# Hybrid decoder layer: transposes and pool matmuls put in groups behind the next stage, TensorE's order written out

## The chip, the cores and the metric

The kernel runs on one core of a Trainium2 chip. Its time is the device time of one execution in microseconds (us); the time of a version is the median of several runs. Five engines work side by side, each through its own queue of instructions in order: TensorE (PE), which multiplies matrices, with its weight loads (PEld) listed apart; VectorE (DVE); ScalarE (ACT); GpSimd (POOL); and SyncE (SP), which issues most loads. An instruction waits at the head of its queue until what it reads is there and what it overwrites is free, and holds up all that stands behind it on that engine.

## What is computed

One decoder layer on 256 tokens of width 2048. The part that matters here, cut from the reference:

```python
h = rms_norm(x, g_mix)
z_pool, z_q, z_kv, z_kr, z_mq = split(h @ w_in)
y_pool = pool_mixer(z_pool, w_pool, pool_scale)    # windowed means, then 4 matrices 128x128
q  = rms_norm(z_q, g_q_lat) @ w_q_up               # 8 heads x (128 plain + 64 rotated)
kv = rms_norm(z_kv, g_kv_lat) @ w_kv_up            # 8 heads x (128 key + 128 value)
# queries and keys: RMS norm per head, rotary part rotated, causal attention
y = concat(y_pool, y_mla, y_mem) @ w_o
x = x + y
x = x + conv_glu_ffn(rms_norm(x, g_ffn))
```

The time is mostly the feed-forward part behind it, which is not edited.

## The kernel before

All matrices are float32. Each weight and each activation is split into a high and a low part, and a product is made of three matmuls. ACT casts the high part of a weight (`wh`, line 98), DVE subtracts it to get the low part (`wl`, line 99), so each chunk of weights passes ACT, then DVE, then PE. Loaded weights (`wr`) have three places, `wh` and `wl` four each. In PSUM there are two sets of four buffers, `psm` for projections and `psa` for the rest.

The stage that is edited lies between the latent projections and the attention scores, at 126 to 182 us of the profile. It runs in the order of lines 643 to 664: `pool_in(0)`, `q_up(2)`, `pool_in(1)`, `kv_up(0)`, `pool_in(2)`, `q_up(0)`, `pool_in(3)`, `pool_mix`, `q_up(1)`, `kv_up(1)`, and then the output projection with the attention heads beside it.

- `pool_in(g)` (lines 539 to 544) projects one of four pool groups: 32 matmuls of line 124, then ACT copies half of the result (line 495), DVE adds the other (line 496) and scales it (line 544).
- `q_up(n)` and `kv_up(n)` (lines 586 and 616) project the latents: 24 matmuls each (lines 159 to 161), token-major. For each half of the tokens (`tt`) ACT copies the result to a tile `tok` and squares it (line 245), DVE sums the squares per head (line 246). Rotated queries (`q_up(2)`) then go through `rotate`, three DVE instructions per half of the rotation (lines 582 to 584). Keys (`kv_up(0)`) are scaled by DVE with their norm (lines 634 to 639). `kv_up(1)` makes the values, which ACT only copies (line 627).
- `to_features` (line 248) turns a finished `tok` tile into feature-major form: four transposes on PE (line 252) into one `psa` buffer, then a copy by ACT (lines 256, 260) or DVE (line 258).
- `pool_mix` (line 547) makes the windowed sums on DVE (lines 553 to 560), and for each group one matmul with the pool weights (line 562) whose result is split by ACT (line 171) and DVE (line 172) into `cat`, the input of the output projection.

`tok` tiles have three places (line 210). The order on each engine is set when the kernel is built: a scheduler places each instruction where it expects its inputs to be ready, except those given to `keep` (line 88), which stay in the order in which they were written among themselves. In this stage only `pool_in(0)` and the heads' matmuls are kept; the transposes, the pool matmuls and the projections around them are placed by the scheduler. So a group of transposes may stand in the middle of another projection's matmuls.

Of the kernel before, what the change touches and what calls it, by code (L numbers as in the profile page):

```python
# [11 lines left out]
F32 = mybir.dt.float32  # L12
# [6 lines left out]
P = 128  # L19
T = 256  # L20
NT = 2
D = 2048
KD = D // P
# [37 lines left out]
def layer(ctx, tc, xT_d, xn_d, memT_d, vec_d, tab_d, w_z_d, w_mqkr_d, w_q_d, w_kv_d, w_mem_d, w_pool_d, w_o_d,  # L61
          w_g_d, w_u_d, w_dn_d, out_d):
    nc = tc.nc
# [8 lines left out]
    def nm(s):  # L72
        uid[0] += 1
        return f"{s}_{uid[0]}"
# [4 lines left out]
    def ps_aux():  # L79
        return psa.tile([P, 512], F32, tag="a", name=nm("psa"))  # L80
# [7 lines left out]
    def keep(ins, on=True):  # L88

        return tc.keep_in_program_order(ins) if on else ins  # L90
# [18 lines left out]
    def gemm_t(ps, raw, o, act, ks, first=True, last=True, kept=False, between=None):  # L109


        ks = list(ks)
        nk = HS // P
        cs = range(0, len(ks), nk)
        for c in cs:
            kc = ks[c:c + nk]

            hi, lo = split_w(raw, o + c * P, len(kc) * P, shift=16 if c // nk % 2 else 48)

            for low in ((False, True) if c // nk % 2 == 0 else (True, False)):  # L120
                for i, k in enumerate(kc):
                    w = (lo if low else hi)[:, i * P:(i + 1) * P]
                    out, m = sides(ps, act(k), low)
                    keep(nc.tensor.matmul(out, w, m,  # L124
                                          start=first and c + i == 0 and not low,
                                          stop=last and c == cs[-1] and i == len(kc) - 1 and low == (c // nk % 2 == 0),
                                          skip_group_check=True), kept)
            if between is not None and c == 0:
                between()
# [51 lines left out]
    identf = const.tile([P, P], F32, name="identf")  # L181
# [14 lines left out]
    mp = mix.enter_context(tc.tile_pool(name="mix", bufs=1))  # L196
# [7 lines left out]
    def sm(n):  # L204
        o = so[0]
        so[0] += n
        return small[:, o:o + n]

    def tok():
        return mp.tile([P, 512], F32, tag="tok", name=nm("tok"), bufs=3)  # L210

    def s4():
        return mp.tile([P, 4, T], F32, tag="s4", name=nm("s4"), bufs=2)
# [31 lines left out]
        nc.scalar.activation(s3, src, AF.Square)  # L245
        nc.vector.tensor_reduce(dst, s3, axis=AX.X, op=ALU.add)

    def to_features(dst, src, tt, n, scale=None, eng=None, bank=ps_aux):

        ps = bank()  # L250
        for i in range(n):
            nc.tensor.transpose(ps[:, i * P:(i + 1) * P], src[:, i * P:(i + 1) * P], identf[:])
        d = dst[:, :, tt * P:(tt + 1) * P]
        p3 = ps[:, :n * P].rearrange("p (i t) -> p i t", t=P)
        if scale is not None:
            nc.scalar.activation(d, p3, AF.Copy, scale=scale)
        elif eng == "v":
            nc.vector.tensor_copy(d, p3)
        else:
            nc.scalar.copy(d, p3)  # L260
# [3 lines left out]
    xg = mp.tile([P, KD, 2 * T], F32R, tag="cat", name="xg")  # L264
# [13 lines left out]
    ps = ps_aux()  # L278
# [25 lines left out]
    for c in range(KD // 2):  # L304
        raw = raw0 if c == 0 else load_w(w_mem_d[c], STG, HS if c == 1 else STG)
# [4 lines left out]
        for i in range(2):  # L310
            k = 2 * c + i
# [3 lines left out]
        if c % 2:  # L315
            h = slice(2 * c - 2, 2 * c + 2)
# [5 lines left out]
    ps = ps_aux()  # L322
# [23 lines left out]
    gqk = sm(2)  # L346
# [38 lines left out]
    for c in range(KD // 2):  # L385
        raw = load_w(w_mqkr_d[c], 2 * 576)
# [97 lines left out]
    def mem_steps(m):  # L484
        if m == 0:
            mq_done()
        for h, step in beside.get(m, ()):
            (mem_heads[h].score, mem_heads[h].turn, mem_heads[h].values)[step]()
        if m == 6:
            latent_scales()  # L490
# [8 lines left out]
    zl = mp.tile([P, 6, 2 * T], F32R, name="zl")  # L499
# [4 lines left out]
    for m in range(6):  # L504
        raw = load_w(w_z_d[m], STG)
        if m in (1, 3):
            keep(nc.sync.dma_start(x1n[:, m // 2, :], xn_d[m // 2]))
        ps = ps_main()
# [6 lines left out]
        else:  # L515
            t = mp.tile([P, T], F32, tag="hadd", name=nm("zsq"), bufs=3)
# [21 lines left out]
    zp = mp.tile([P, 4, T], F32, name="zp")  # L538
    def pool_in(g):
        raw = load_w(w_z_d[6 + g], STG)  # L540
        ps = ps_main()
        gemm_t(ps, raw, 0, lambda k: xg[:, k, :], range(KD), kept=g == 0, between=lambda: mem_steps(6 + g))
        half_add(zp[:, g, :], ps)
        nc.vector.tensor_tensor(zp[:, g, :], zp[:, g, :], rxb[:], op=ALU.mult)


    def pool_mix():
        wp = tok()
        nc.scalar.dma_start(wp[:], w_pool_d)
        cur, w = zp, 1  # L550
        for g in range(4):
            nxt = s4()
            nc.vector.tensor_copy(nxt[:, g:4, 0:w], cur[:, g:4, 0:w])
            nc.vector.tensor_tensor(nxt[:, g:4, w:T], cur[:, g:4, w:T], cur[:, g:4, 0:T - w], op=ALU.add)
            cur = nxt
            w *= 2
            s = cur[:, g, :]
            e = TAB["edge"][0] + 16 * g
            nc.vector.tensor_tensor(s[:, 0:16], s[:, 0:16], tab[:, e:e + 16], op=ALU.mult)
            nc.vector.scalar_tensor_tensor(zp[:, g, :], s, 1.0 / w, zp[:, g, :], op0=ALU.mult, op1=ALU.subtract)  # L560
            ps = ps_aux()
            nc.tensor.matmul(ps[:, 0:T], wp[:, g * P:(g + 1) * P], zp[:, g, :], start=True, stop=True)
            split_act(cat[:, g, :], ps[:, 0:T], v("pool_scale", g))


# [2 lines left out]
    qnT, knT, krT, qrT = qkv[:, 0:8], qkv[:, 8:16], qkv[:, 16:24], mqT  # L568
# [6 lines left out]
    def rotate(dst, src, s, tt, nh):  # L575
# [5 lines left out]
        for a, b, (ra, rb), op, o in ((x1, x2, (r[0], r[1]), ALU.subtract, 0), (x2, x1, (r[2], r[3]), ALU.add, 32)):  # L581
            nc.vector.tensor_tensor(t[:, 0], a, ra, op=ALU.mult)
            nc.vector.tensor_tensor(t[:, 1], b, rb, op=ALU.mult)
            nc.vector.tensor_tensor(dst[:, :, o:o + 32], t[:, 0], t[:, 1], op=op)

    def q_up(n):
        raw = load_w(w_q_d[n], STG)
        pss = [[ps_main()[:]] for _ in range(NT)]
        for i in range(2):
            hi, lo = split_w(raw, i * HS, HS)  # L590
            gemm_n(pss, hi[:].rearrange("p (k n) -> p k n", n=512), lo.rearrange("p (k n) -> p k n", n=512),
                   zl, 2 * i, i == 0, i == 1)
        for tt in range(NT):
            ps = pss[tt][0]
            t = tok()
            if n < 2:
                nc.scalar.copy(t[:], ps)
                head_sq(ssq_n[:, tt, 4 * n:4 * n + 4], t[:].rearrange("p (h d) -> p h d", d=NOPE))
                to_features(qnT[:, 4 * n:4 * n + 4], t, tt, 4, gqk[:, 0:1])
            else:  # L600
                t1 = tok()
                nc.scalar.copy(t1[:], ps)
                p3 = t1[:].rearrange("p (h d) -> p h d", d=ROPE)
                head_sq(ssq_r[:, tt, :], p3)
                rotate(t[:].rearrange("p (h d) -> p h d", d=ROPE), p3, 0, tt, H)
                to_features(qrT, t, tt, 4)

# [6 lines left out]
    def kv_up(n):  # L616
        raw = load_w(w_kv_d[n], STG)
        for h in range(2):
            pss = [[ps_main()[:]] for _ in range(NT)]
            hi, lo = split_w(raw, h * HS, HS)  # L620
            gemm_n(pss, hi[:].rearrange("p (k n) -> p k n", n=512), lo.rearrange("p (k n) -> p k n", n=512),
                   zl, 4, True, True)
            for tt in range(NT):
                ps = pss[tt][0]
                p3 = ps.rearrange("p (h d) -> p h d", d=128)
                if n == 1:
                    nc.scalar.activation(vv[:, tt, 4 * h:4 * h + 4, :], p3, AF.Copy, scale=skv[:, tt:tt + 1])
                    continue
                t = tok()
                t3 = t[:].rearrange("p (h d) -> p h d", d=NOPE)  # L630
                o = slice(tt * H + 4 * h, tt * H + 4 * h + 4)
                nc.scalar.copy(t[:], ps)
                head_sq(fk[:, o], t3)
                nc.vector.tensor_scalar(fk[:, o], fk[:, o], skv2[:, tt:tt + 1], sskr[:, tt:tt + 1],
                                        op0=ALU.mult, op1=ALU.add)
                rsqrt_(fk[:, o], fk[:, o], 1.0 / QK)
                nc.vector.tensor_scalar(fkn[:, o], fk[:, o], skv[:, tt:tt + 1], None, op0=ALU.mult)
                nc.vector.tensor_scalar(fkr[:, o], fk[:, o], rx[:, tt:tt + 1], None, op0=ALU.mult)
                nc.vector.tensor_tensor(t3, t3, fkn[:, o].unsqueeze(2).to_broadcast([P, 4, NOPE]), op=ALU.mult)
                to_features(knT[:, 4 * h:4 * h + 4], t, tt, 4, None, "v")  # L640


    pool_in(0)
    q_up(2)
    pool_in(1)
    kv_up(0)
    pool_in(2)
    q_up(0)
    pool_in(3)
    cat = mp.tile([P, KD, 2 * T], F32R, tag="cat", name="cat")  # L650
    pool_mix()
    q_up(1)

    fq = sm(NT * H)
# [7 lines left out]
                                op0=ALU.mult, op1=ALU.mult)  # L662

    kv_up(1)

    def rope_keys():
        for tt in range(NT):
# [264 lines left out]
    for c in range(2):  # L932
# [3 lines left out]
        for j in range(PAIRS):  # L936
            kept = c > 0 or j > SEVEN[0]
# [4 lines left out]
            else:  # L942
                between = None
                if j == 0 and done is not None:
                    between = lambda o=done: finish(0, o, nc.gpsimd)
                elif j >= PAIRS - 2:
                    between = lambda s=j - PAIRS + 3: common(c, com, s)
# [89 lines left out]
```

## Time and profile before

| | |
|---|---|
| median of 3 runs | 1004.26 us (1003.88 to 1004.4) |
| the profiled execution's own time | 1004.01 us |
| its span, first to last instruction | 1002.2 us |
| PE busy | 995.9 us, 99% |
| DVE busy | 767.6 us, 77% |
| ACT busy | 586.5 us, 59% |
| edited stage, 116 to 182 us: PE, DVE, ACT busy | 65.92, 55.54, 44.50 us |

A row of the timeline or of the chain of waits gives the start and the length in us, then engine, line and tile. "x4" is the number of instructions merged. In square brackets stands how long the engine was idle before, and what ended that. Rows on DVE and ACT overlap by about 0.1 us with the next one, so the distance between two starts is what an instruction costs its engine. Lines are those of the kernel before; in the changed one they are up to 17 higher.

### The profile page before, as it was taken

How to read it: one execution, taken by the hardware profiler on the slowest of the kernel's cores; microseconds unless marked ns; L12 is line 12 of the kernel's file. 1: busy time of each engine (PE TensorE's matmuls, PEld its weight loads, DVE VectorE, ACT ScalarE, POOL GpSimd, SP SyncE). 2: the span in 40 equal slices, each digit the busy share in tenths (PEclk: the TensorE clock that was granted, in tenths of full speed). 3: DMA queues.
4: the chain of work that ended last, by engine and by line, in shares of the span. 5: the costliest groups of instructions: out<-in, count | busy, mean ns of one | idle time of the engine just before them, and what ended most of it. 6: DMA issues, size and time to landing. Idle time of an engine off the chain costs nothing.

```text
span 1002.2 us, 14014 instructions
## 1 busy us (share of the span) xinstructions
PE 995.9 (99%) x5338; PEld 858.4 (86%) x5338; DVE 767.6 (77%) x1160; ACT 586.5 (59%) x859; POOL 18.5 (2%) x39
## 2 busy tenths in 40 slices
PE   9999999999999999999999999999999999999998
PEld 7898888888888888888888888888888888888886
DVE  6778689855677777777776767777677998899887
ACT  7678666544576555555555655555565656545562
POOL 1000000000000000000000000000000000010000
PEclk9999999999999999999999999999999999999999
DMA  9867443433654555555555555555556666486651
GB/s 359 293 247 268 159 172 143 166 129 129 235 224 169 192 195 201 174 204 187 192 201 193 194 176 204 192 186 208 190 191 221 223 229 210 168 294 213 222 195 43
DMA packets 31764, 200.17 MB, mean 200 GB/s; under 512 B 3664, under 2 KB 4176, under 8 KB 9808
## 3 DMA queue, kind: packets, MB, share of 16 engines
q1 hardware_dynamic: 28512, 189.04, 52.8%
q0 software_dynamic: 2752, 9.44, 2.8%
q8 instruction: 42, 0.69, 0.3%
q10 hardware_dynamic: 432, 0.79, 0.2%
q14 instruction: 26, 0.21, 0.1%
HBM read 195.06 MB, written 4.19 MB: 199 GB/s over the span
## 4 chain that ended last, share of the span: by engine, by line
PE 96%; DVE 2%; issue 1%; DMA 0%; ACT 0%; DVEq 0%; ACTq 0%
PE psm L142 47%; PE psm L124 7%; PE psm L159 5%; PE psm L161 5%; PE psm L160 5%; PE psa L867 3%; PE psa L865 3%; PE psm L867 3%; PE psm L865 3%; PE psa L866 3%; PE psm L866 3%; DVE wl L99 1%; PE psa L688 1%; PE psa L159 1%; PE psa L161 1%
## 5 line engine op out<-in xcount | busy, mean ns | idle before, releaser
L99 DVE TENSOR_TENSOR wl<-wr,wh 128x1024 fp32r<-128x1024 f32 (+2 forms) x338 | 391.5, 1172 | 130.6 <-ACT wh L98 74.2
L98 ACT CAST wh<-wr 128x1024 fp32r<-128x1024 f32 (+2 forms) x338 | 340.5, 1012 | 132.6 <-PE psm L142 55.4
L142 PE MATMUL psm<-h,wh 128*128 128x512 f32 x1376 | 320.1, 390 | 0.0
L142 PEld LDWEIGHTS psm<-h,wh 128*128 128x128 f32 x1376 | 255.1, 188 | 51.2
L142 PEld LDWEIGHTS psm<-h,wl 128*128 128x128 f32 x1376 | 163.8, 188 | 3.3
L142 PE MATMUL psm<-h,wl 128*128 128x256 f32 x1376 | 164.5, 277 | 0.0
L98 ACT CAST wh<-dn 128x1024 fp32r<-128x1024 f32 (+1 forms) x66 | 65.4, 995 | 79.5 <-PE psa L866 32.1
L99 DVE TENSOR_TENSOR wl<-dn,wh 128x1024 fp32r<-128x1024 f32 (+1 forms) x66 | 74.0, 1147 | 16.0 <-ACT wh L98 16.0
L802 ACT ACTIVATE gc<-g,vec 128x256 f32<-128x256 f32 x44 | 26.5, 602 | 93.3 <-DVE g L800 93.3
L804 DVE SCALAR_TENSOR_TENSOR gc<-g,vec,gc 128x255 f32<-128x255 f32 x88 | 42.5, 483 | 32.9 <-ACT gc L802 31.4
L124 PE MATMUL psm<-xg,wh 128*128 128x512 f32 x160 | 39.9, 393 | 0.0
L159 PE MATMUL psm<-wh,cat 128*128 128x512 f32 x96 | 38.2, 398 | 0.0
L161 PE MATMUL psm<-wl,cat 128*128 128x512 f32 x96 | 37.4, 390 | 0.0
L160 PE MATMUL psm<-wh,cat 128*128 128x512 f32 x96 | 37.4, 389 | 0.0
L866 PE MATMUL psa<-wh,aT 128*128 128x512 f32 x88 | 34.3, 390 | 0.0
L865 PE MATMUL psa<-wh,aT 128*128 128x512 f32 x88 | 34.3, 389 | 0.0
L866 PE MATMUL psm<-wh,aT 128*128 128x512 f32 x88 | 34.2, 389 | 0.0
L865 PE MATMUL psm<-wh,aT 128*128 128x512 f32 x88 | 34.2, 389 | 0.0
L867 PE MATMUL psa<-wl,aT 128*128 128x512 f32 x88 | 33.9, 389 | 0.0
L124 PEld LDWEIGHTS psm<-xg,wh 128*128 128x128 f32 x160 | 29.1, 188 | 5.4
L867 PE MATMUL psm<-wl,aT 128*128 128x512 f32 x88 | 33.3, 389 | 0.0
L794 ACT COPY g<-psm 128x256 f32<-128x256 f32 x44 | 16.5, 374 | 27.7 <-PE psm L142 27.7
(234 smaller groups left out, 1418.5 us busy)
## 6 DMA issues: line engine op xcount, KB each, us to landing
wr<-in_w_g SPq DMA_DIRECT2D x44, 1024.0 KB, 4.8
wr<-in_w_u SPq DMA_DIRECT2D x44, 1024.0 KB, 4.8
wr<-in_w_dn SPq DMA_DIRECT2D x33, 1024.0 KB, 4.8
wr<-in_w_o SPq DMA_DIRECT2D x16, 1024.0 KB, 4.8
dn<-in_w_dn SPq DMA_DIRECT2D x11, 1024.0 KB, 4.8
wr<-in_w_z SPq DMA_DIRECT2D x10, 1024.0 KB, 6.8
wr<-in_w_mem SPq DMA_DIRECT2D x6, 1024.0 KB, 8.4
wr<-in_w_mqkr SPq DMA_DIRECT2D x8, 576.0 KB, 5.0
```

Of the source, the lines that this page charges most:

```text
L98: keep(nc.scalar.copy(hi[:, c:e], raw[:, o + c:o + e]), kept)
L99: keep(nc.vector.tensor_tensor(lo[:, c:e], raw[:, o + c:o + e], hi[:, c:e].bitcast(F32), op=ALU.subtract), kept)
L124: keep(nc.tensor.matmul(out, w, m, start=first and c + i == 0 and not low, stop=last and c == cs[-1] and i == len(kc) - 1 and low == (c // ...
L142: nc.tensor.matmul(o, parts[k // nk][low][:, i * P:(i + 1) * P], m, start=k == 0 and low == (s == 1), stop=k == KD - 1 and low == (s == 0) ...
L159: keep(nc.tensor.matmul(ps, xh, hi[:, i, o], start=first and i == 0, stop=False), kept)
L160: keep(nc.tensor.matmul(ps, xl, hi[:, i, o], start=False, stop=False), kept)
L161: keep(nc.tensor.matmul(ps, xh, lo[:, i, o], start=False, stop=last and i == nk - 1), kept)
L802: nc.scalar.activation(gc[:], g[:], AF.Identity, bias=v("conv_b", f), scale=v("cw2", f))
L804: nc.vector.scalar_tensor_tensor(gc[:, d:T], g[:, 0:T - d], v(w, f), gc[:, d:T], op0=ALU.mult, op1=ALU.add)
L865: nc.tensor.matmul(ps, a[0], b[0], start=first, stop=False)
L866: nc.tensor.matmul(ps, a[1], b[0], start=False, stop=False)
L867: nc.tensor.matmul(ps, a[0], b[1], start=False, stop=last)
```

## The change

Five edits. `tok` gets five places. `pool_in` is kept for all four groups, and so are the matmuls of `q_up` and `kv_up`. Finished `tok` tiles are no longer turned at once: `to_features` calls are collected in a list `due`, and `turn_due()` writes out all that are collected, kept, after the `pool_in` that follows. `pool_mix` only makes the sums; the four pool matmuls move to `pool_out`, kept, which is called after `kv_up(1)`, with the last `turn_due()` behind it. What is computed, and with how many instructions of each kind, stays the same.

```diff
     def tok():
-        return mp.tile([P, 512], F32, tag="tok", name=nm("tok"), bufs=3)
+        return mp.tile([P, 512], F32, tag="tok", name=nm("tok"), bufs=5)
...
-    def to_features(dst, src, tt, n, scale=None, eng=None, bank=ps_aux):
+    def to_features(dst, src, tt, n, scale=None, eng=None, bank=ps_aux, kept=False):
...
-            nc.tensor.transpose(ps[:, i * P:(i + 1) * P], src[:, i * P:(i + 1) * P], identf[:])
+            keep(nc.tensor.transpose(ps[:, i * P:(i + 1) * P], src[:, i * P:(i + 1) * P], identf[:]), kept)
...
-        gemm_t(ps, raw, 0, lambda k: xg[:, k, :], range(KD), kept=g == 0, between=lambda: mem_steps(6 + g))
+        gemm_t(ps, raw, 0, lambda k: xg[:, k, :], range(KD), kept=True, between=lambda: mem_steps(6 + g))
...
+        return wp
+
+    def pool_out(wp):
+        for g in range(4):
             ps = ps_aux()
-            nc.tensor.matmul(ps[:, 0:T], wp[:, g * P:(g + 1) * P], zp[:, g, :], start=True, stop=True)
+            keep(nc.tensor.matmul(ps[:, 0:T], wp[:, g * P:(g + 1) * P], zp[:, g, :], start=True, stop=True))
             split_act(cat[:, g, :], ps[:, 0:T], v("pool_scale", g))
...
+    due = []
+
+    def turn_due():
+        for args in due:
+            to_features(*args, kept=True)
+        due.clear()
...
     pool_in(0)
     q_up(2)
     pool_in(1)
+    turn_due()
     kv_up(0)
     pool_in(2)
+    turn_due()
     q_up(0)
     pool_in(3)
+    turn_due()
     cat = mp.tile([P, KD, 2 * T], F32R, tag="cat", name="cat")
-    pool_mix()
+    wp = pool_mix()
     q_up(1)
...
     kv_up(1)
+    pool_out(wp)
+    turn_due()
```

How the queues stand, at three places. First PE at the end of `pool_in(1)`, before (the last matmuls of `pool_in(1)` and the transposes of the first tile of rotated queries, `tok_209`, then `kv_up(0)`):

```order
L124 MATMUL psm_220_1456<-xg_84,wl_224_1478 128x256 x8
L124 MATMUL psm_220_1456<-xg_84,wh_223_1477 128x512 x7
L252 MATMUL psa_213_1429<-identf_68,tok_209_1416 128x128 x4
L124 MATMUL psm_220_1456<-xg_84,wh_223_1477 128x512
L159 MATMUL psm_227_1503<-wh_229_1505,zl_839 128x512
```

And the same place now, where `tok_213` is the second tile of rotated queries:

```order
L124 MATMUL psm_218_1444<-xg_84,wl_222_1466 128x256 x8
L124 MATMUL psm_218_1444<-xg_84,wh_221_1465 128x512 x8
L252 MATMUL psa_224_1489<-identf_68,tok_209_1416 128x128 x4
L252 MATMUL psa_225_1495<-identf_68,tok_213_1429 128x128 x4
L159 MATMUL psm_227_1503<-wh_229_1505,zl_839 128x512
```

The second tile's transposes came after fourteen matmuls of `kv_up(0)` before; now all of `kv_up(0)` stands behind them.

Second, DVE in the stretch that scales the keys, before (`wl` are weights' low parts, `hsq` squares, `tok_241` and `tok_244` the last two key tiles, `qkv` the turned queries and keys):

```order
L639 TENSOR_TENSOR tok_241_1573<-tok_241_1573,small_82 128x512
L634 TENSOR_SCALAR small_82<-small_82 128x4
L496 TENSOR_TENSOR zp_1289<-hadd_253_1650,psm_248_1609 128x256
L192 RECIPROCAL small_82<-small_82 128x4
L99 TENSOR_TENSOR wl_270_1716<-wr_267_1712,wh_269_1715 128x1024
L258 COPY qkv_1290<-psa_243_1584 128x4x128
L637 TENSOR_SCALAR small_82<-small_82 128x4
L638 TENSOR_SCALAR small_82<-small_82 128x4
L639 TENSOR_TENSOR tok_244_1590<-tok_244_1590,small_82 128x512
```

And now, where the last two key tiles are `tok_239` and `tok_241`:

```order
L651 TENSOR_TENSOR tok_239_1561<-tok_239_1561,small_82 128x512
L646 TENSOR_SCALAR small_82<-small_82 128x4
L99 TENSOR_TENSOR wl_260_1675<-wr_254_1654,wh_259_1674 128x1024
L192 RECIPROCAL small_82<-small_82 128x4
L496 TENSOR_TENSOR zp_1289<-hadd_249_1626,psm_244_1585 128x256
L649 TENSOR_SCALAR small_82<-small_82 128x4
L650 TENSOR_SCALAR small_82<-small_82 128x4
L651 TENSOR_TENSOR tok_241_1572<-tok_241_1572,small_82 128x512
L544 TENSOR_TENSOR zp_1289<-zp_1289,rxb_837 128x256
L258 COPY qkv_1290<-psa_250_1630 128x4x128
```

The copies of turned keys (line 258) have moved behind the last key tile. One subtract of line 99 still stands in the stretch, an earlier chunk's (`wl_260`) in place of `wl_270`; `wl_260` stood further ahead before.

Third, PE at the end of `kv_up(1)` now (line 566 are the pool matmuls, `tok_286` and `tok_288` the last query tiles, `psm_305` the first of the output projection):

```order
L161 MATMUL psm_296_1858<-wl_298_1860,zl_839 128x512
L566 MATMUL psa_299_1877<-zp_1289,tok_274_1760 128x256
L566 MATMUL psa_300_1881<-zp_1289,tok_274_1760 128x256
L566 MATMUL psa_301_1885<-zp_1289,tok_274_1760 128x256
L566 MATMUL psa_302_1889<-zp_1289,tok_274_1760 128x256
L252 MATMUL psa_303_1893<-identf_68,tok_286_1818 128x128 x4
L252 MATMUL psa_304_1899<-identf_68,tok_288_1823 128x128 x4
L159 MATMUL psm_305_1905<-wh_308_1909,cat_1759 128x512
```

The pool matmuls stood one by one among the last 25 projection matmuls before (one of `q_up(1)`, then `kv_up(1)`), and the last transposes right behind the fourth pool matmul.

More of the change, by code (lines that the diff above doesn't have):

```diff
@@ L591, in q_up @@
             gemm_n(pss, hi[:].rearrange("p (k n) -> p k n", n=512), lo.rearrange("p (k n) -> p k n", n=512),
-                   zl, 2 * i, i == 0, i == 1)
+                   zl, 2 * i, i == 0, i == 1, True)
         for tt in range(NT):
@@ L598, in q_up @@
                 head_sq(ssq_n[:, tt, 4 * n:4 * n + 4], t[:].rearrange("p (h d) -> p h d", d=NOPE))
-                to_features(qnT[:, 4 * n:4 * n + 4], t, tt, 4, gqk[:, 0:1])
+                due.append((qnT[:, 4 * n:4 * n + 4], t, tt, 4, gqk[:, 0:1]))
             else:
@@ L605, in q_up @@
                 rotate(t[:].rearrange("p (h d) -> p h d", d=ROPE), p3, 0, tt, H)
-                to_features(qrT, t, tt, 4)
+                due.append((qrT, t, tt, 4))
     sskr, fk, fkn, fkr = sm(NT), sm(NT * H), sm(NT * H), sm(NT * H)
@@ L621, in kv_up @@
             gemm_n(pss, hi[:].rearrange("p (k n) -> p k n", n=512), lo.rearrange("p (k n) -> p k n", n=512),
-                   zl, 4, True, True)
+                   zl, 4, True, True, True)
             for tt in range(NT):
@@ L639, in kv_up @@
                 nc.vector.tensor_tensor(t3, t3, fkn[:, o].unsqueeze(2).to_broadcast([P, 4, NOPE]), op=ALU.mult)
-                to_features(knT[:, 4 * h:4 * h + 4], t, tt, 4, None, "v")
+                due.append((knT[:, 4 * h:4 * h + 4], t, tt, 4, None, "v"))
     pool_in(0)
```

## The prediction

> **What bounds the kernel now.** I read the page first, for which engine has no time left, then the table by stage, the waits and the chain of waits of the stage that is edited.
>
> ```profile
> span 1002.2 us, 14014 instructions
> ...
> PE 995.9 (99%) x5338; PEld 858.4 (86%) x5338; DVE 767.6 (77%) x1160; ACT 586.5 (59%) x859; POOL 18.5 (2%) x39
> ...
> PEclk9999999999999999999999999999999999999999
> ```
>
> TensorE (PE) is busy for 99% of the span, with the top digit of granted clock in every slice. So a microsecond that PE loses is a microsecond of the kernel, and other engines matter only where PE waits for them. The edited stage, from the table by stage (PE, PEld, DVE, ACT, POOL, clock, DMA):
>
> ```profile
> 116.00:182.00 66.00, 65.92 (x352) 55.29 (x351) 55.54 (x117) 44.50 (x72) 0.00 (x0) 1.00 0.46 162
> ```
>
> PE works in 65.92 of 66.00 us, but VectorE (DVE) has only a sixth of slack. What PE's weight loads wait for between 120 and 182 us:
>
> ```profile
> PEld psa L252 <- DVE tok L639: 0.7, 2, 0.5
> PEld psa L252 <- DVE tok L584: 0.4, 1, 0.4
> PEld psa L562 <- PE psm L160: 0.4, 1, 0.4
> PEld psa L252 <- issue: 0.2, 1, 0.2
> PEld psa L252 <- ACT tok L597: 0.2, 1, 0.2
> ```
>
> They are transposes (L252) and a pool matmul (L562) for which the data was just late. From the chain of waits, where a piece runs from the end of the one before to its own end:
>
> ```profile
> 116.28 5.53 PE psm L124 x32
> ...
> 126.35 0.23 PE psm L159
> ...
> 131.79 5.27 PE psm L124 x31
> ...
> 137.08 0.66 PE psa L252 x4
> 137.74 0.23 PE psm L124
> ...
> 141.18 0.44 PE psa L252 x4
> ...
> 148.09 0.66 PE psa L252 x4
> ...
> 160.19 3.35 PE psm L124 x21
> ...
> 170.61 0.43 PE psa L562 x2
> ...
> 174.45 0.87 PE psa L252 x8
> ...
> 182.41 2.73 PE psa L688 x18
> ```
>
> A group of four transposes costs 0.44 us, or 0.66 if it was waited for; eight cost 0.87, so grouping by itself saves nothing. An up-projection (24 matmuls) takes 131.79 - 126.35 = 5.44 us, a pool projection (32) 5.53, a pool matmul 0.43. **All that can be gained:** from 126.35 to the first scores at 182.41 are 56.06 us. The work in it: five up-projections 27.20, three pool projections 16.59, 48 transposes (40 of L252, 8 of the rope keys) at 0.109 = 5.22, four pool matmuls 1.72, 18 output matmuls at 5.44/24 = 0.227, 4.08. Sum 54.81: the waits cost 1.25 us now.
>
> **The change part by part.** Nothing is added or removed. The transposes and pool matmuls move on PE, and PE takes its queue in the order written. Before, a group came where its data was ready; now each stands behind the next stage whether its data is ready or not, with all later matmuls queued behind it. So for each group I ask when its data is there and when PE arrives. From a row's end to the end of the group that waited for it: L639 below ends at 147.35 + 0.69 = 148.04, the group of 148.09 ends at 148.75, so 0.71 us.
>
> *First group, rotated queries, behind pool_in(1).* PE is through pool_in(1) at 131.79 + 5.53 = 137.32, through the first four transposes at 137.76, and could end the second four at 138.20. They read a tile whose last rotation (L584) DVE finishes late:
>
> ```profile
> 136.61 0.42 DVE L584 TENSOR_TENSOR tok<-rt 128x256 f32<-128x256 f32 x1
> ...
> 137.61 1.22 DVE L99 TENSOR_TENSOR wl<-wr,wh 128x1024 fp32r<-128x1024 f32 x1
> ...
> 140.42 0.42 DVE L584 TENSOR_TENSOR tok<-rt 128x256 f32<-128x256 f32 x1
> 140.76 2.35 DVE L99 TENSOR_TENSOR wl<-wr,wh 128x1024 fp32r<-128x1024 f32 x2
> 143.03 1.46 DVE L246 TENSOR_REDUCE small<-hsq 128x4 f32<-128x512 f32 x2
> ```
> ```profile
> 136.61:140.84 4.23, 4.21 (x22) 3.16 (x20) 4.23 (x12) 2.57 (x5) 0.00 (x0) 1.00 0.58 230
> ```
>
> DVE is busy for all 4.23 us up to 140.84, and its order up to there is the same in both programs. So the group ends at 140.84 + 0.71 = 141.55: **3.35 us lost**. Before, these four stood behind fourteen matmuls of kv_up(0) (the piece at 141.18) and cost 0.44.
>
> *Second group, four key tiles, behind pool_in(2).* PE: kv_up(0) ends at 141.55 + 5.44 = 146.99, pool_in(2) at 152.52, four groups could end at 154.28. The keys' path:
>
> ```profile
> 140.08 0.59 ACT L632 COPY tok<-psm 128x512 f32<-128x512 f32 x1 [0.50 <-PE psm L161]
> 140.56 1.05 ACT L98 CAST wh<-wr 128x1024 fp32r<-128x1024 f32 x1
> ```
> ```profile
> 145.22 1.23 DVE L99 TENSOR_TENSOR wl<-wr,wh 128x1024 fp32r<-128x1024 f32 x1 [0.34 <-ACT wh L98]
> ...
> 147.35 0.69 DVE L639 TENSOR_TENSOR tok<-tok,small 128x512 f32<-128x512 f32 x1
> ...
> 149.71 0.69 DVE L258 COPY qkv<-psa 128x512 f32<-128x512 f32 x1
> 150.32 0.17 DVE L192 RECIPROCAL small<-small 128x4 f32<-128x4 f32 x1
> ...
> 154.56 0.69 DVE L639 TENSOR_TENSOR tok<-tok,small 128x512 f32<-128x512 f32 x1
> ```
>
> ScalarE (ACT) copies the first tile 140.08 - 137.97 = 2.11 us after kv_up(0) starts (137.74 + 0.23 = 137.97), so at 143.66. The cast behind it on ACT starts 0.48 later and ends at 145.19. DVE's next subtract needs that cast, so DVE idles until then and cannot use PE's first stall to get ahead. Before, from that subtract (the second of the pair at 140.76, so 141.90) to the end of the last L639 at 155.25, DVE took 13.35 us. Of these go three copies (L258, 0.61 from start to start), a subtract (1.13, half of 143.03 - 140.76) that now stand later, and the 0.34 wait: 10.05 stay. The last tile is ready at 155.24 and its group ends at 155.95: **1.67 us lost**.
>
> *Third group, query tiles, behind pool_in(3).* They are ready: the waits there go.
>
> *Pool matmuls and last queries, behind kv_up(1).* Six outputs ask for the four buffers psa, so the fifth, a group of transposes, must wait until both halves of the first pool output (ACT's L171, DVE's L172) are read out. PE from 155.95: q_up(0) 5.44 and pool_in(3) 5.53 end at 166.92, eight transposes 167.79, q_up(1) and kv_up(1) 178.67, four pool matmuls 180.39, and the group could end at 180.83. DVE:
>
> ```profile
> 163.99 0.42 DVE L496 TENSOR_TENSOR zp<-hadd,psm 128x256 f32<-128x256 f32 x1 [0.88 <-ACT hadd L495]
> ...
> 170.83 0.48 DVE L172 SCALAR_TENSOR_TENSOR cat<-psa,vec,cat 128x256 fp32r<-128x256 f32 x1
> 171.22 0.16 DVE L559 TENSOR_TENSOR s<-s,tab 128x16 f32<-128x16 f32 x1
> ...
> 179.33 0.68 DVE L678 COPY qkv<-psa 64x512 f32<-64x512 f32 x1
> ```
> ```profile
> 163.99:179.33 15.34, 15.31 (x76) 12.50 (x75) 15.12 (x37) 12.27 (x20) 0.00 (x0) 1.00 0.27 87
> ```
>
> pool_in(3) ended at 160.19 + 3.35 = 163.54, L496 started 0.45 later, and from there to L678 DVE was busy for 15.12 us. The same rows now come before the first L172, without the four L172 that lay between (4 x 0.39): 13.56, and the first L172 0.48. It ends at 166.92 + 0.45 + 14.04 = 181.41, the transposes at 182.12: **1.29 us lost**. ACT gets there earlier.
>
> What follows is covered: the output projection's first matmuls read the first two pool outputs, whose L172 are done by then; the rope-key copies (L678, four of them) end before the scores ask. Five places for tok take waits for free places away and add none. The loads stand in the same order on SP's queue and lead by a buffer or more. The pool weights' load stands on ACT's queue behind the copy of q_up(0)'s second result as before; q_up(0) ends at 161.39 and the first matmul that needs the load comes at 178.67. Each is put at nothing; a load without its lead would cost at most the stage's slack, some tenths.
>
> **Sum:** 3.35 + 1.67 + 1.29 = 6.31, less the 1.25 of today: 5.06 us. On the profiled execution's 1004.01 that is 1009.07; the median of the runs is 0.25 above it, so 1009.3. The step from "ready" to "group ends" and the DVE chains are read to some tenths each: alone, this case has 1008.2 to 1010.4.
>
> **The rivals.**
> *Only the first stall.* While PE stands, DVE and ACT catch up, and the later groups find their data ready. For it: DVE's queue is short of work at 141.9. Against: the next row on DVE hangs on a cast that ACT does only after a copy of kv_up(0)'s own result. 3.35 - 1.25 = 2.1, so 1006.4. Chance 0.12.
>
> *The clock falls.* In the first stall PE runs no ordinary matmul from 137.32 to 141.55, 4.23 us. In this trace PE waits for nothing that long after the start, and every slice has the top digit of the clock, so its rows can't price it: nothing at least; at most kv_up(0) takes twice its 5.44. I take half of it at half speed: 2.72 more on PE. The key tiles come up to 2.1 later, so the second stall shrinks by 0.6: 1011.4. Chance 0.09. The Trainium skill, "TensorE: Matmul & The Clock Gate", section "Why this matters for your kernels", speaks against the change here: gaps of more than about 3 us between bursts of matmuls bring the clock down to half. By its window of 3.4 us that would be 1.7 us more, an estimate; that page's part on transposes adds that they don't count as busy in the same way. No row here shows either.
>
> *Faster.* Every group finds its data ready, since a whole stage lies ahead of it, and the 1.25 us of waits goes: 1003.0. This decides itself on the first group: it holds if the last L584 ends before 137.7, and DVE is 3.1 us behind that with no idle time in the 4.23 us before. Chance 0.04.
>
> *No difference.* DVE falls back less than the order says, since the rows that came from a busy trace get shorter, and the stalls come to some 1 to 3 us: 1004.0 to 1006.0. DVE's rows repeat to 0.02 us, which speaks against it. Chance 0.06.
>
> **How the numbers follow.** The forecast has 0.69. With the rival of one stall it holds 0.81, so the range is 1006.3 to 1011.5, which takes in most of the clock's case too. Some 0.2%, 2 us, is what a measurement of this kernel can tell from no change. The rival of one stall lies so near it that I give 0.02 of it to no difference: faster 0.04, same 0.08, slower 0.88.
>
> **What would show it.** In the profile after, PE should wait in L252 for DVE's last rotation about 3.3 us, for the key scaling about 1.7 us, and behind the pool matmuls for L172 about 1.2 us, with all of DVE's rows as long as now, the granted clock at 1.00 and the scores starting near 187.5. I am wrong if PE is through the first group before 139, if the second or third stall is missing, or if the matmuls after a stall take longer than 0.23 us each.

## The result and the profile after

The changed kernel takes 1011.21 us (median of 4 runs, 1010.77 to 1012.29), the kernel before 1004.07 us on the same chip (4 runs, 1003.84 to 1004.40). The ratio is 1.0073, 95% interval 1.0061 to 1.0085: slower by 7.1 us. The profiled execution took 1011.51 us, 7.50 more than that of before. The page, in the rows that answer to those of before:

```profile
span 1009.7 us, 14014 instructions
...
PE 997.5 (99%) x5338; PEld 860.3 (85%) x5338; DVE 767.4 (76%) x1160; ACT 586.6 (58%) x859; POOL 18.5 (2%) x39
...
PEclk9999999999999999999999999999999999999999
```

The instructions and DVE's busy time are those of before, and the span is 7.5 us longer. PE's busy time grew by 1.6 us with the same 5338 instructions, so some of them took longer. The row of the granted clock can't show it: a slice is 25 us, and 9 means 90% or more. The waits of PE between 120 and 192 us (total, times, longest):

```profile
PE psa L252 <- DVE tok L588: 3.2, 1, 3.2
PE psa L252 <- DVE tok L651: 1.5, 1, 1.5
PE psa L252 <- DVE cat L172: 1.1, 1, 1.1
```

These are the three waits of the prediction, each for the named instruction of DVE (the lines have moved by the diff: L588 is the rotation, L651 the scaling of a key tile). The small waits of before, five rows, are gone. The same three on PE's timeline (start, length, then the idle time before):

```profile
137.75 0.60 PE L252 MATMUL psa<-identf,tok 128*128 128x128 f32 x4
141.51 1.09 PE L252 MATMUL psa<-identf,tok 128*128 128x128 f32 x4 [3.15 <-DVE tok L588]
142.25 0.78 PE L159 MATMUL psm<-wh,zl 128*128 128x512 f32 x1
142.82 0.63 PE L160 MATMUL psm<-wh,zl 128*128 128x512 f32 x1
143.25 0.63 PE L161 MATMUL psm<-wl,zl 128*128 128x512 f32 x1
...
145.21 0.40 PE L160 MATMUL psm<-wh,zl 128*128 128x512 f32 x1
145.45 0.40 PE L161 MATMUL psm<-wl,zl 128*128 128x512 f32 x1
...
149.09 1.07 PE L124 MATMUL psm<-xg,wh 128*128 128x512 f32 x4
```
```profile
154.59 1.47 PE L252 MATMUL psa<-identf,tok 128*128 128x128 f32 x12
157.60 0.63 PE L252 MATMUL psa<-identf,tok 128*128 128x128 f32 x4 [1.53 <-DVE tok L651]
```
```profile
180.82 1.89 PE L566 MATMUL psa<-zp,tok 128*128 128x256 f32 x8
183.77 1.09 PE L252 MATMUL psa<-identf,tok 128*128 128x128 f32 x8 [1.06 <-DVE cat L172]
```

And there is a fourth thing. After the first wait the group of four takes 1.09 us where a waited-for group took 0.66 before, and the first matmuls of kv_up(0) come 0.43 us apart (142.82 to 143.25), the later ones 0.24 (145.21 to 145.45). The table by stage has the reason in its column of the granted clock, the number behind the five engines:

```profile
138.00:142.00 4.00, 0.85 (x7) 0.61 (x6) 4.00 (x9) 1.75 (x3) 0.00 (x0) 0.95 0.55 229
142.00:144.00 2.00, 2.00 (x7) 1.71 (x6) 0.59 (x1) 0.59 (x1) 0.00 (x0) 0.50 0.42 57
144.00:146.00 2.00, 2.00 (x8) 1.53 (x8) 0.00 (x0) 0.12 (x1) 0.00 (x0) 0.75 0.80 332
146.00:148.00 2.00, 2.00 (x11) 1.64 (x10) 0.55 (x1) 2.00 (x4) 0.00 (x0) 1.00 0.32 135
```

The granted clock was at half in 0.4 of the first 4 us, in the whole of the next 2 and in 1 of the 2 behind them: 3.4 us in all. The first row also shows DVE busy for all 4.00 us while PE works for 0.85: PE stands because DVE is at work.

### The profile page after: what moved, and what is told of

It reads as the page before. It is cut to its first block, busy times and chain, and to the rows that moved or that the text cites. A ratio compares the mean times of both kernels' runs of the same rounds, so it can differ in the third digit from the quotient of the medians.

```text
span 1009.7 us, 14014 instructions
## 1 busy us (share of the span) xinstructions
PE 997.5 (99%) x5338; PEld 860.3 (85%) x5338; DVE 767.4 (76%) x1160; ACT 586.6 (58%) x859; POOL 18.5 (2%) x39
## 4 chain that ended last, share of the span: by engine, by line
PE 79%; DVE 4%; issue 1%; ACT 1%; DVEq 0%; ACTq 0%
PE psm L142 47%; PE psm L159 3%; PE psa L882 3%; PE psm L161 3%; PE psa L884 3%; PE psm L160 3%; PE psm L884 3%; PE psa L883 3%; PE psm L882 3%; PE psm L883 3%; DVE wl L99 2%; PE psm L124 2%; PE psa L705 1%; DVE dn L943 0%; PE psa L776 0%
```

## The experiments

The theory at the outset: PE takes a written order, three groups are written ahead of their data, and each costs what DVE is late; 3.15 us of empty PE then halve the clock for a short time. The rivals are two. The five places for tok, or the order in itself, may cost something; then moving single groups gives back less. Or the long matmuls have another cause than the empty PE; then filling the wait doesn't help. All kernels are edits of the changed one unless it is said otherwise. Where `turn_due(n)` stands, it turns only the first n of the groups that are due. "The stage" is measured from the first matmul of `q_up(2)` to the scores, and "the opening" is all that lies ahead of it; the stage took 56.22 us before (126.19 to 182.41) and 63.09 us in the changed kernel (126.81 to 189.90). Each ran beside the kernel before (medians 1003.98, 1004.09 and 1003.99 in the three series).

**The rotated queries' groups behind kv_up(0).**

```diff
     pool_in(1)
-    turn_due()
     kv_up(0)
+    turn_due(2)
     pool_in(2)
     turn_due()
```

> The rotated queries' two groups are turned behind kv_up(0) instead of in front of it; nothing else moves. Theory (three late groups, and a clock that falls after the first, long wait): the first wait goes, with it the slow matmuls (1.7 us), granted clock 1.00 all through. The keys are then up to 2.3 us nearer to PE, so their waits grow to about 3 us in all, the pool's stays at 1.1 to 1.3. Some 4 us less than the changed kernel: about 1007. Rival (the time is lost to the grouping itself, or to an order of DVE that the five places brought): about 1011, as the changed kernel.

Measured: 1006.63 us (7 runs, 1006.42 to 1007.82), ratio 1.0027 (1.0016 to 1.0038). The waits of PE:

```profile
PE psa L252 <- DVE small L649: 1.5, 1, 1.5
PE psa L252 <- DVE cat L172: 1.1, 1, 1.1
PE psa L252 <- DVE tok L651: 0.2, 1, 0.2
```

With two groups moved the kernel is 4.6 us faster than the changed one. The first wait is gone, the second is now split over the last two key tiles, the third stands. PE is idle for 2.8 us, and three groups that were waited for cost 0.22 more each (0.66 against 0.44); less the 1.25 of before, that is 2.2. The stage took 58.43 us in the profiled execution, 2.21 more than before. The rest of the 2.65 between the medians lies ahead of the stage, in the opening (below). The clock was 0.999 or 1.00 in six runs; the seventh, 1007.82 with 0.998, is left open.

**The first wait filled with matmuls.** Fourteen more matmuls of 512 columns ahead of the second group, into the buffer that the transposes then fill; their product is not used (pad is 14 for that group and 0 for all others).

```diff
+        for _ in range(pad):
+            keep(nc.tensor.matmul(ps[:], xg[:, 0, 0:P], xg[:, 0, :], start=True, stop=True))
```

> The changed kernel with 14 extra matmuls of 512 columns in front of the second group of transposes, written to the buffer that the transposes then fill; their product is not used. They fill the 3.2 us in which PE waits. Theory (the clock falls because PE stands still): the group still ends when DVE is done, the clock stays at 1.00, kv_up(0) takes 5.44 instead of 6.66 us and the group is 0.44 shorter: about 1.7 us less than the changed kernel, 1009.5. Rival (the slow matmuls have another cause, such as weights or buffers that come late): kv_up(0) stays at 6.7 us, about 1011 or a little more.

Measured: 1009.40 us (4 runs, 1009.14 to 1009.78), ratio 1.0054 (1.0039 to 1.0069). On PE's timeline:

```profile
138.01 3.42 PE L252 MATMUL psa<-xg 128*128 128x512 f32 x14
141.41 0.66 PE L254 MATMUL psa<-identf,tok 128*128 128x128 f32 x4
141.82 0.48 PE L159 MATMUL psm<-wh,zl 128*128 128x512 f32 x1
142.14 0.40 PE L160 MATMUL psm<-wh,zl 128*128 128x512 f32 x1
142.37 0.40 PE L161 MATMUL psm<-wl,zl 128*128 128x512 f32 x1
```

The group ends when it did (141.41 + 0.66 = 142.07, against 142.60 with the half clock in it), and kv_up(0)'s matmuls come 0.23 apart. The clock was 0.999 or 1.00 in all four runs. Fourteen useless matmuls make the kernel 1.8 us faster (1.3 against the later series of the changed kernel, 1010.70), and the stage took 61.49 us, 1.60 less than in the changed kernel. So the long matmuls came from the empty PE.

**The same with transposes.** Twenty-eight transposes of the identity in place of the fourteen matmuls, their product not used either.

```diff
+            keep(nc.tensor.transpose(ps[:, 0:P], identf[:], identf[:]))
```

> As the run with extra matmuls, but the wait is filled with 28 extra transposes of the identity, 0.109 us each, into the same buffer. Theory (any work of PE holds the clock): as with matmuls, about 1009.5, clock 1.00. Rival (transposes do not count as work, as the Trainium skill's page TensorE: Matmul & The Clock Gate says): the clock falls as in the changed kernel, about 1011.

Measured: 1009.58 us (4 runs, 1009.47 to 1009.85), ratio 1.0056 (1.0040 to 1.0073):

```profile
137.89 3.22 PE L252 MATMUL psa<-identf 128*128 128x128 f32 x28
141.21 0.66 PE L254 MATMUL psa<-identf,tok 128*128 128x128 f32 x4
```

The same as with matmuls: the clock, 0.999 or 1.00 in all four runs, held with nothing but transposes in the wait.

**Half of the wait filled.** Seven of those matmuls, so that some 1.6 us stay empty; their product is not used.

> The changed kernel with 7 extra matmuls of 512 columns in the first wait (1.6 us), so that some 1.6 of its 3.2 us stay empty. The product is not used. Theory (the clock falls only after a long stretch without work): 1.00 in nearly all runs and about 1009.4, as with 14 matmuls. Rival (any wait at this place lets it fall): 0.998 and about 1011 in most runs.

Measured: 1009.44 us (5 runs, 1009.20 to 1009.68), ratio 1.0054 (1.0040 to 1.0067):

```profile
137.46 1.83 PE L252 MATMUL psa<-xg 128*128 128x512 f32 x7
140.86 0.66 PE L254 MATMUL psa<-identf,tok 128*128 128x128 f32 x4 [1.57 <-DVE tok L590]
```

1.57 us without work left the clock as it was: 0.999 or 1.00 in all five runs.

**The last groups ahead of the pool matmuls.**

```diff
     kv_up(1)
-    pool_out(wp)
     turn_due()
+    pool_out(wp)
```

> The last group of transposes stands in front of the four pool matmuls instead of behind them. Theory (the third wait is for a buffer of psa that the first pool output holds until L172): the 1.1 to 1.3 us at the transposes go; 0.3 us come back where the fourth pool matmul waits for a buffer of the transposes, and up to 0.4 where the scores wait for the rope keys: about 0.5 to 0.9 us less than the changed kernel, 1010.4. Rival (the output projection's first matmuls would wait for the same L172 anyway): no change, 1011.2.

Measured: 1008.54 us (4 runs, 1008.25, 1008.51, 1008.58 and 1009.96), ratio 1.0048 (1.0033 to 1.0063). The expected time held for one run only, the fourth, with a mean clock of 0.998. (Half clock for 3.4 of some 1010 us makes a mean of 0.998.) In the other three the clock stayed at 1.00, though the same wait was there:

```profile
140.99 0.66 PE L252 MATMUL psa<-identf,tok 128*128 128x128 f32 x4 [3.15 <-DVE tok L588]
141.40 0.48 PE L159 MATMUL psm<-wh,zl 128*128 128x512 f32 x1
141.72 0.39 PE L160 MATMUL psm<-wh,zl 128*128 128x512 f32 x1
141.95 0.40 PE L161 MATMUL psm<-wl,zl 128*128 128x512 f32 x1
```

So the clock doesn't fall in every run. The third wait is worth about what the theory says: against the filled wait, where the clock holds too, 1009.40 - 1008.54 = 0.9 us. The edit takes away 1.06 of idle time and 0.22 of the waited-for group, and brings two waits of weight loads of 0.3 us each, the ones that the kernel with all three moves shows below.

**The places alone.** The kernel before with five places for tok.

```diff
-        return mp.tile([P, 512], F32, tag="tok", name=nm("tok"), bufs=3)
+        return mp.tile([P, 512], F32, tag="tok", name=nm("tok"), bufs=5)
```

> The kernel before with five places for tok and nothing else. Theory (the places do no harm, the order on PE does): within 0.3 us of the kernel before, 1004.0, unless copies to tok run ahead and reorder DVE. Rival (the places move something that costs): 1006 or more.

Measured: 1004.31 us (11 runs), before 1004.09 (27 runs), ratio 1.0002 (0.9994 to 1.0011). That rival falls.

**The changed kernel once more**, unchanged, since the clock had not fallen in every run.

> The changed kernel once more, to see how often the clock falls after the first wait. Theory (whether it falls is chance, since one of four runs with the same wait fell where the last group stood first, and four of four here): two groups of times, about 1009.5 with clock 1.00 and about 1011.1 with 0.998. Rival (it always falls in this program): all near 1011.

Measured: 1010.70 us (5 runs: 1010.70, 1011.00, 1010.59 and 1010.90 with a mean clock of 0.998, 1009.21 with 0.999), ratio 1.0063 (1.0049 to 1.0076). The one run that kept its clock lies at the time of the filled waits, 1.6 us below the others.

**Only the keys' groups later.** Behind q_up(0) in place of pool_in(2); the first and the last places as in the change.

```diff
     pool_in(2)
-    turn_due()
     q_up(0)
+    turn_due(4)
     pool_in(3)
     turn_due()
```

> The changed kernel with only the keys' four groups moved, behind q_up(0) instead of in front of it. Theory (the second wait is a loss of its own, 1.7 us): 1.8 us less than the changed kernel in runs of the same clock, so 1007.7 where the clock holds and 1009.2 where it falls. Rival (DVE carries the delay on, and PE waits later instead): the third wait grows by as much and the time stays at 1009.5 to 1011.

Measured: 1009.39 us (5 runs, 1007.65 to 1010.60), ratio 1.0051 (1.0039 to 1.0064). The run with a clock of 0.999 took 1007.65, the others (0.996 to 0.998) 1008.92 to 1010.60. The second wait is gone, and the first and third are as they were:

```profile
PE psa L252 <- DVE tok L588: 3.2, 1, 3.2
PE psa L252 <- DVE cat L172: 1.1, 1, 1.1
```

Between runs that kept their clock it gives 1009.40 (the filled wait) - 1007.65 = 1.75 us, from a single run; the second wait was 1.73.

**All three moves together**, to see whether the order was at fault or writing an order at all: the rotated queries' and the keys' groups one stage later, and the last groups ahead of the pool matmuls.

```diff
     pool_in(1)
-    turn_due()
     kv_up(0)
+    turn_due(2)
     pool_in(2)
-    turn_due()
     q_up(0)
+    turn_due(4)
     pool_in(3)
     turn_due()
...
     kv_up(1)
-    pool_out(wp)
     turn_due()
+    pool_out(wp)
```

> Every group one more matmul stage later: rotated queries behind kv_up(0), keys behind q_up(0), plain queries behind pool_in(3), the last queries in front of the pool matmuls. Theory (each loss was a group that stood in front of its data): all three waits go, some 0.3 us remain at the fourth pool matmul and up to 0.4 at the rope keys: 0.6 to 1.0 us less than the kernel before, 1003.2, clock 1.00. Rival (DVE is the bound of the stage, so a wait only moves): 1005 or more, with waits for DVE at other places.

Measured: 1003.20 us (11 runs, 1003.03 to 1003.55), ratio 0.9991 (0.9982 to 0.9999). All that is left of waits there are two of the weight loads:

```profile
PEld psm L160 <- DVE cat L172: 0.3, 1, 0.3
PEld psa L566 <- ACT qkv L256: 0.3, 1, 0.3
```

The first comes because the output projection now stands right behind the pool matmuls, whose results DVE must still copy. Hence the last kernel.

**The pool matmuls between the halves of kv_up(1)**, in the loop over its two halves, and the rest as in the one above.

```diff
-                   zl, 4, True, True, True)
+                   zl, 4, True, True, True); n == 1 and h == 0 and pool_out(wp)
...
     kv_up(1)
     turn_due()
-    pool_out(wp)
```

> As the run with every group one stage later, but the four pool matmuls stand between the halves of kv_up(1), where DVE has just made the last pool sum. Theory: L172 then comes before the two subtracts that were in front of it, no group waits for a buffer of psa, and the whole 1.25 us of waits and drains in the kernel before is gained: 1002.8. Rival (the pool matmuls wait for the last sum here): 0.5 us or more back, 1003.3 or above.

Measured: 1002.95 us (11 runs, 1002.67 to 1003.17), ratio 0.9988 (0.9979 to 0.9997): 1.1 us faster than the kernel before and 7.8 us faster than the changed kernel in the same series (1010.70). Its table by stage has no idle PE in the stage:

```profile
116.00:182.00 66.00, 66.00 (x361) 57.03 (x360) 56.77 (x119) 44.67 (x72) 0.00 (x0) 1.00 0.48 171
```

From the chain of waits of the kernel before (whose scores start at 182.41), and then of this one:

```profile
123.46 2.89 PE psm L124 x16
```
```profile
123.75 2.89 PE psm L124 x16
...
181.51 3.00 PE psa L705 x20
```

From the second half of pool_in(0) to the scores it was 182.41 - 123.46 = 58.95 us, now 181.51 - 123.75 = 57.76: 1.19 us gained of the 1.25 that the prediction found to be all there was.

## Why the prediction was right, and what its likeliest case left out

Term by term, from PE's timeline and the chain of waits of the changed kernel (the prediction's numbers in the second column). The first wait is given without the half clock, which has a row of its own. The terms leave 0.11 of the measured 6.87 unassigned.

```
term                                        predicted   measured
first wait, rotated queries behind pool_in(1)   3.35      3.34
second wait, key tiles behind pool_in(2)        1.67      1.73
third wait, behind the pool matmuls             1.29      1.28
today's waits, gone                            -1.25     -1.25
half clock behind the first wait                  -       1.66
sum                                             5.06      6.76
scores start later by, within the stage                   6.87
opening, ahead of the stage                       -       0.62
```

- **First wait: right.** Four transposes end at 141.51 + 1.09 = 142.60; without a wait they would at 138.20 + 0.62 (the trace is that much later before the stage begins) = 138.82. Of these 3.78 us, 0.44 is the clock (1.09 against 0.66). DVE's last rotation starts at 141.04, 140.42 + 0.62 to the hundredth: DVE's chain repeated, as the prediction counted on. The move of these groups alone took the wait away.
- **Second wait: right, and with its reason.** Three of four groups end at 156.06, the fourth could at 156.50 and did at 157.60 + 0.63 = 158.23. DVE could not use PE's first stall to get ahead, because its next subtract hangs on a cast that ACT does only after its copy of kv_up(0)'s result:

```profile
141.37 1.21 DVE L99 TENSOR_TENSOR wl<-wr,wh 128x1024 fp32r<-128x1024 f32 x1
147.45 1.23 DVE L99 TENSOR_TENSOR wl<-wr,wh 128x1024 fp32r<-128x1024 f32 x1 [4.86 <-ACT wh L98]
```

  DVE stood 4.86 us there. That is why the rival of only one stall fell.
- **Third wait: right.** Eight transposes behind the four pool outputs (180.82 + 1.89 = 182.71, and 0.87) could end at 183.58 and ended at 184.86. The chain names the copy that freed the buffer, the first L172 at 183.33.
- **Left out of the likeliest case: the clock.** The prediction's likeliest case said that the granted clock stays at 1.00 and that matmuls after a stall come 0.23 us apart. It named the contrary as what would make it wrong, and the contrary happened: 0.44 us in the group, and kv_up(0) from 142.60 to 149.26 on PE's timeline, 6.66 where the prediction counted 5.44, 1.22 more. The direction and the range held; what came true is the rival to which it gave 0.09, with 1011.4 for a measured 1011.21. That this number is so near is in part luck, since two errors in it partly cancel. It took 2.72 us for the clock where 1.66 was measured, and took 0.6 off the second wait, which did not shrink: the keys pass through the slowed kv_up(0) as well, so that ACT's first copy of them came 3.28 us after kv_up(0) began (142.60 to 145.88) and not 2.11.

```profile
145.88 0.59 ACT L644 COPY tok<-psm 128x512 f32<-128x512 f32 x1 [2.66 <-PE psm L161]
```

- The step that failed was to price the fall by the absence of rows. The trace of before has no such wait after its start, so it said nothing for the clock's holding either, and in the runs with this wait the clock fell in 13 of 18. A chance of 0.09 was too little. The Trainium skill, "TensorE: Matmul & The Clock Gate", section "Why this matters for your kernels", warns of gaps of more than about 3 us. The trace agrees with that rule at 3.15 us, though not in every run, and its 1.66 us agree with the estimate of 1.7 us that the prediction worked out from that page.
- **Put at nothing: right as far as it was tried.** Five places for tok alone: 1004.31 against 1004.09, with a stage of 56.26 us against 56.22. Nothing behind the stage changed: from the start of the scores to the end of the span it is 1009.7 - 189.90 = 819.8 us, before 1002.2 - 182.41 = 819.8.
- **The opening, 0.62 us**, was in no term, and it is no fixed cost of the change. PE's first projection matmul stands at 5.59 in place of 5.40, and another, some 12 us in, waits 0.25 longer. But in the second profiled execution of the same changed kernel the stage begins at 126.02, earlier than before, and takes 63.01 us, as in the first (63.09). What the opening varies with was not followed further.

**Open.** Why the clock falls in some runs and not in others of the same wait. The Trainium skill, "TensorE: Matmul & The Clock Gate", section "Part 1: The HAM clock gate (the "warmup" mystery)", speaks of a free-running window of activity, by which it would hang on where the wait begins in that window; no run here set that phase, so it wasn't tried. What the traces do show is that the fall has no fixed distance from the start of the wait. It came 3.2 us after PE's last transpose in the first profiled execution of the changed kernel, 3.5 in the second, and 2.9 with only the keys' groups later; the half clock lasted 3.4 us each time. In the last of these PE was still waiting when it came:

```profile
137.09 0.60 PE L252 MATMUL psa<-identf,tok 128*128 128x128 f32 x4
140.85 1.11 PE L252 MATMUL psa<-identf,tok 128*128 128x128 f32 x4 [3.16 <-DVE tok L588]
```
```profile
140.00:142.00 2.00, 1.15 (x5) 1.15 (x6) 1.93 (x4) 0.00 (x0) 0.00 (x0) 0.64 0.00 0
142.00:144.00 2.00, 2.00 (x6) 1.52 (x6) 0.00 (x0) 0.59 (x1) 0.00 (x0) 0.51 0.45 119
```

A mean of 0.64 over 2 us is half clock for 1.44 us, so from 140.56 on, 0.29 us before PE had work again. Nor is it settled why one run of the kernel with only the keys' groups later (1010.60, clock 0.996) lost more than one such fall, or why one run of the first experiment (1007.82, clock 0.998) lost 1.2 us: that experiment's profiled execution, another run, shows no wait over 1.5 us.

## What to carry to other kernels

Where an engine is given a written order, each place in it is a promise that the data is there. Read from the trace when the producer's queue (here DVE's) reaches the last instruction that the group needs, and put the group behind the first stage that ends later: one stage more here turned 7 us lost into 1 us gained. Where outputs share a few buffers, ask too which engine empties each one, and when. And if a stall of an otherwise busy TensorE comes to about 3 us, count the slow matmuls behind it as a term of the sum; where the stall can't be removed, matmuls or transposes put into it kept the clock here, and filling half of it was enough.

## What the runs showed of the chip

- With 3.15 us without work on PE the granted clock fell to half in 13 of 18 runs (8 of 9 of the changed kernel, 1 of 4 with the last groups first, 4 of 5 with the keys later, counted by a mean clock of 0.998 or less), for 3.4 us in each of the three profiled executions that show it, at a cost of about 1.6 us (1.66 in the table above, 1.60 by the stage of the filled wait). With that wait half or wholly filled it fell in 0 of 13. The one exception to "no long wait, no fall" is the run of the first experiment (1 of 7) named under Open; with five places alone and in the last two kernels it fell in 0 of 33.
- Transposes of fp32 kept the clock as matmuls did: 28 of them in the wait gave 1009.58 us and a full clock in 4 of 4 runs. The Trainium skill, "TensorE: Matmul & The Clock Gate", section "Part 4: PE-mode transpose", says that transposes don't count as work in the same way, beside figures for bf16. For fp32 transposes that hold a clock already full, the measurement here decides against it; whether they would also bring the full clock about was not tried.
